# Mixer A of a two-layer trunk: left and right key tiles' blocks folded by a minimum before the exponential and put apart by GpSimd, and q and k split straight from PSUM

## The chip, the cores and the metric

The kernel is one program on one core of a Trainium2 chip. The metric is the time in device microseconds (us) of one execution. The core has five engines that run their own instruction lists and wait for each other by semaphores: PE (TensorE: matrix products, and transposes as a product with a unit matrix), DVE (VectorE), ACT (ScalarE), POOL (GpSimd) and SP (SyncE, which here only issues transfers). PE writes its results into PSUM, a small memory from which DVE and ACT read them; everything else lies in SBUF.

## The reference, cut to what matters

The trunk has two layers on 1024 tokens of width 1024 (a grid of 16 rows and 64 columns). The change touches only mixer A, the first layer's attention over a neighbourhood: each query sees a window of 8 rows and 16 columns around it.

```
def mixer_a(h, w_in, rpb, w_out):
    proj = h @ w_in
    q, k, v, gate = jnp.split(proj, 4, axis=-1)          # 16 heads of 64
    ...
    bias = rpb[:, dr[:, None, :, None], dc[None, :, None, :]]
    ...
        kg = jnp.take(k, flat, axis=2)...                 # the 8 x 16 window's keys
        sc = jnp.einsum('bhqd,bhqnd->bhqn', qb, kg).astype(jnp.float32) * scale
        sc = sc + bb.astype(jnp.float32)[None]
        pr = jax.nn.softmax(sc, axis=-1).astype(vg.dtype)
        return jnp.einsum('bhqn,bhqnd->bhqd', pr, vg)
    ...
    return (o * jax.nn.silu(gate)) @ w_out
```

## The kernel before, in words

The tokens are laid out as 8 tiles of 128: tile j holds 8 columns of the grid with their 16 rows. With a window of 16 columns, the queries of tile j find their keys in the tiles j-1, j and j+1 (the inner tiles j = 1 to 6) or in two tiles (j = 0 and 7). Within the left and the right tile, a query's window takes complementary columns: a key column that counts on the left does not count on the right.

Every matrix product of fp32 numbers is made as three products of high and low parts (`split3`, `mm` on line 317), so each operand is first split: ACT writes the rounded high part, DVE subtracts it from the original and writes the low part.

Mixer A is one long stretch of the span. It goes through 128 steps, 16 heads h by 8 query tiles j, and step n = (h, j) issues in this order: a head (a Y finish `fin` on POOL if one is due; at j = 1 the five POOL operations of `table(h+1)`, line 681; at other j one job, a DMA issued by POOL or SP), then

- `f_T(n)`: PE transposes the three 128 x 128 blocks of exponentials `sp` into PSUM tile `t` (line 723), ACT evacuates the high part into `PTh` (line 726), DVE the low part into `PTl` (line 727); both buffers have a slot for each pair of key and query tile;
- `f_E(n+1)`: ACT exponentials over 384 columns, in place in `sp` (line 715);
- `f_S(n+2)`: PE scores into `s`, 384 columns, and one DVE instruction that adds mask and bias and takes the row minimum (line 706);
- `f_AV(n-2)`: PE products of V with three slots of `PTh`, then of `PTl`, into `o`. In the heads 3, 7 and 11 each of them is followed by one tile of the v projection (`v_items`, 24 matmuls of 256 columns into a tile `d`, evacuated by ACT line 633 and DVE line 634).

`mix()` deals the dense work between these items by a cost table: in each head 8 items of the next head's q and k projection (two halves, each with a PSUM tile `d` of its own, 24 matmuls of 512 columns) and 4 items of the gate projection (one `d`). All of these share the two buffers of the PSUM pool `pd`. After every item `pulse()` runs: it pumps the weight queue (which loads `wstage` and has ACT line 226 and DVE line 231 split it into `wh` and `wl`) and counts down `post`, a list of things to issue so many pulses later. Each engine works through its list in the order in which the program issues it.

When a half of q and k stands in `d`, `qk_evac` copies it to SBUF (`th`, line 647) and splits it from there in three posted parts, after 2, 5 and 8 pulses (`QD = (2, 5, 8)`): ACT q high and k high (650, 651), then DVE q low and k low (654, 655) and a copy of k high to the other 64 partitions (656), then the copy of k low (659). For head 0 all of it is issued at once.

The Y path of a head pair is joined on ACT and DVE (lines 497 and 461), its reciprocals go through DRAM and come back as `rb` by two transfers of SP (line 470), and `fin` multiplies on POOL: by the gate (line 531), then by `rb` (line 532). Of the finishes, 14 lie on steps of mixer A, at j = 3 and j = 6 of the even heads.

Of the kernel before, what the change touches and what calls it, by code (L numbers as in the profile page):

```python
# [11 lines left out]
F32 = mybir.dt.float32  # L12
F32R = mybir.dt.float32r
# [74 lines left out]
def lay_out(inp):  # L88
# [46 lines left out]
    ok = np.stack([rowok, left, rowok, right, rowok], axis=1)  # L135
    mask = np.where(ok, 0.0, BIG).astype(np.float32)

    inv = np.power(np.float32(10000.0), -np.arange(16, dtype=np.float32) * np.float32(2.0) / np.float32(32.0)).astype(np.float32)
# [7 lines left out]
    def swap(v):  # L146
# [5 lines left out]
        "x": tokens(g["x"][0]), "wts": W, "rpb": rpb, "gains": gains, "hgains": hg,  # L152
        "mask": mask, "rope": np.stack([cosT, sinT], axis=1),
        "gain0": gains[0].reshape(8, 128).T,
# [3 lines left out]
@with_exitstack  # L158
def trunk(ctx, tc, x, wts, rpb, gains, hgains, mask, rope, gain0, out):
    nc = tc.nc  # L160
# [446 lines left out]
    def mixer_a():  # L607
        jobs = weight_sums()
        with ExitStack() as es:
# [27 lines left out]
            def qk_evac(h, hf):  # L637
                def evac(ps):
                    if hf == 0:
                        QS[h] = qkp.tile([128, 1024], F32R, name="QS")  # L640
                        KA[h] = qkp.tile([128, 1024], F32R, name="KA")
                        KB[h] = qkp.tile([128, 1024], F32R, name="KB")
                    s = slice(hf * 512, (hf + 1) * 512)
                    lo, hi = slice(0, 64), slice(64, 128)
                    qs, ka, kb = QS[h], KA[h], KB[h]
                    raw = sb.tile([128, 512], F32, name="th", bufs=2)
                    act.activation(raw, ps, AF.Copy)

                    def one():
                        act.activation(qs[lo, s], raw[lo], AF.Copy, scale=-0.125)  # L650
                        act.activation(ka[hi, s], raw[hi], AF.Copy)

                    def two():
                        dve.scalar_tensor_tensor(qs[hi, s], raw[lo], -0.125, qs[lo, s], op0=ALU.mult, op1=ALU.subtract)
                        dve.tensor_tensor(kb[hi, s], raw[hi], ka[hi, s], ALU.subtract)
                        dve.tensor_copy(ka[lo, s], ka[hi, s])
# [29 lines left out]
            def near(j):  # L686
                return max(j - 1, 0), min(j + 1, NT - 1)

            def f_S(h, j):
# [12 lines left out]
                else:  # L702
# [5 lines left out]
                                         scale=1.0, scalar=1e38, op0=ALU.add, op1=ALU.min, accum_out=mn)  # L708
                SP[h, j] = (sp, mn)

            def f_E(h, j):
                k0, k1 = near(j)
                n = (k1 - k0 + 1) * 128
                sp, mn = SP[h, j]
                act.activation(sp[:, :n], sp[:, :n], AF.Exp, bias=mn, scale=-1.0, accum_out=RS[h][:, j:j + 1])

            def f_T(h, j):
                k0, k1 = near(j)
                m = k1 - k0 + 1
                sp, _ = SP.pop((h, j))  # L720
                ps = psT.tile([128, 4, 128], F32, name="t")
                for i in range(m):
                    pe.transpose(ps[:, i], sp[:, i * 128:(i + 1) * 128], ident)
                f0 = k0 * 3 + (j - k0 + 1)
                sl = slice(f0, f0 + 2 * m - 1, 2)
                act.activation(PTh[:, sl], ps[:, :m], AF.Copy)  # L726
                dve.tensor_tensor(PTl[:, sl], ps[:, :m], PTh[:, sl], ALU.subtract)  # L727

# [125 lines left out]
            newton(4)  # L854
            sync.dma_start(MK, mask)
            for c in range(8):
                sync.dma_start(U[:, c], rpb[:, :, 7 - c:31 - c])
# [27 lines left out]
            ptp = es.enter_context(tc.tile_pool(name="ptp", bufs=1))  # L885
            PTh = ptp.tile([128, NT * 3, 128], F32R, name="PTh")
            PTl = ptp.tile([128, NT * 3, 128], F32R, name="PTl")
            for d in qk_items(0):
# [20 lines left out]
            for h in range(NH):  # L909
                att = []  # L910
                for j in range(NT):
# [783 lines left out]

NAMES = ["x", "wts", "rpb", "gains", "hgains", "mask", "rope", "gain0"]

# [14 lines left out]
```

## Time and profile before

| what | value |
|---|---|
| median of 3 runs | 1530.34 us (1529.68 to 1532.05) |
| profiled execution's own time | 1530.75 us |
| its span | 1529.0 us (1.75 us lie outside) |
| PE, DVE, ACT, POOL busy | 98%, 72%, 59%, 20% of the span |
| granted TensorE clock, mean | 0.999 |
| mixer A's steps | about 70 to 520 us of the span |

The profile is of one execution. Busy time counts an engine as busy while an instruction of it runs; a matmul's end is modelled, so PE's starts tell more than its durations: where matmuls start every 0.23 us without a gap, PE is full, though each is shown as lasting 0.39. "Idle before" and the waits name the instruction whose end let an engine go on. The dense phase, mixer B and the last dense phase follow mixer A; the change does not touch them.

### The profile page before, as it was taken

How to read it: one execution, taken by the hardware profiler on the slowest of the kernel's cores; microseconds unless marked ns; L12 is line 12 of the kernel's file. 1: busy time of each engine (PE TensorE's matmuls, PEld its weight loads, DVE VectorE, ACT ScalarE, POOL GpSimd, SP SyncE). 2: the span in 40 equal slices, each digit the busy share in tenths (PEclk: the TensorE clock that was granted, in tenths of full speed). 3: DMA queues.
4: the chain of work that ended last, by engine and by line, in shares of the span. 5: the costliest groups of instructions: out<-in, count | busy, mean ns of one | idle time of the engine just before them, and what ended most of it. 6: DMA issues, size and time to landing. Idle time of an engine off the chain costs nothing.

```text
span 1529.0 us, 24364 instructions
## 1 busy us (share of the span) xinstructions
PE 1499.0 (98%) x8976; PEld 1312.1 (86%) x8976; DVE 1099.1 (72%) x2091; ACT 899.6 (59%) x1801; POOL 305.0 (20%) x413
## 2 busy tenths in 40 slices
PE   9999999999999999999999999999999999999997
PEld 8888988988988887888988889989899888778786
DVE  7666576477477499767877786777877777689856
ACT  6565465466366635433567776666767777744432
POOL 1222232242112000010312132443131300000022
PEclk9999999999999999999999999999999999999999
DMA  8325355262122863262210111111111122663123
GB/s 261 129 85 135 83 142 162 63 169 80 36 87 73 327 247 97 90 203 79 75 49 22 32 40 49 46 32 51 49 32 43 45 69 81 226 224 114 67 88 134
DMA packets 91096, 157.22 MB, mean 103 GB/s; under 512 B 18144, under 2 KB 54112, under 8 KB 90464
## 3 DMA queue, kind: packets, MB, share of 16 engines
q1 hardware_dynamic: 85824, 139.66, 27.4%
q0 software_dynamic: 2560, 8.39, 3.1%
q10 hardware_dynamic: 2592, 7.61, 1.4%
q8 instruction: 71, 1.16, 0.3%
q14 instruction: 49, 0.40, 0.1%
HBM read 125.10 MB, written 50.83 MB: 115 GB/s over the span
## 4 chain that ended last, share of the span: by engine, by line
PE 36%; DVE 10%; ACT 4%; issue 3%; DMA 0%; SPq 0%; ACTq 0%; DVEq 0%
PE d L317 17%; PE o L317 7%; PE t L1178 5%; PE s L317 5%; DVE PTl L1181 2%; DVE mn L1162 1%; ACT P L1168 1%; ACT PTh L1180 1%; PE t L317 1%; DVE xn L1498 1%; DVE QS L1142 0%; DVE wl L231 0%; DVE X L1394 0%; PE t L1132 0%; ACT wh L226 0%
## 5 line engine op out<-in xcount | busy, mean ns | idle before, releaser
L317 PE MATMUL d<-wh,HTh 128*128 128x256 f32 (+1 forms) x1032 | 343.0, 334 | 3.6 <-ACT HTh L446 0.8
L317 PE MATMUL d<-wh,HTl 128*128 128x256 f32 (+1 forms) x1032 | 337.9, 329 | 0.3 <-DVE HTl L447 0.3
L317 PE MATMUL d<-wl,HTh 128*128 128x256 f32 (+1 forms) x1032 | 337.2, 329 | 0.0
L1181 DVE TENSOR_TENSOR PTl<-t,PTh 128x512 fp32r<-128x512 f32 x256 | 164.4, 684 | 111.6 <-ACT PTh L1180 111.2
L317 PEld LDWEIGHTS d<-wh,HTh 128*128 128x128 f32 x1032 | 194.6, 189 | 24.3 <-ACT HTh L446 1.2
L317 PEld LDWEIGHTS d<-wl,HTh 128*128 128x128 f32 x1032 | 194.8, 190 | 18.9
L317 PEld LDWEIGHTS d<-wh,HTl 128*128 128x128 f32 x1032 | 194.7, 190 | 18.7 <-DVE HTl L447 0.5
L317 PE MATMUL d<-HTh,wh 128*128 128x512 f32 x504 | 206.0, 409 | 0.0
L317 PE MATMUL d<-HTh,wl 128*128 128x512 f32 x504 | 198.4, 394 | 0.0
L317 PE MATMUL d<-HTl,wh 128*128 128x512 f32 x504 | 197.6, 392 | 0.0
L1168 ACT ACTIVATE P<-s,mn 128x1024 f32<-128x1024 f32 x128 | 142.7, 1115 | 59.7 <-DVE mn L1162 59.0
L1180 ACT ACTIVATE PTh<-t 128x512 fp32r<-128x512 f32 x256 | 140.0, 593 | 44.6 <-PE t L1178 44.3
L1162 DVE TENSOR_REDUCE mn<-s 128x1 f32<-128x1024 f32 x128 | 154.8, 1210 | 12.3 <-PE s L317 12.2
L1178 PE MATMUL t<-ident,P 128*128 128x128 f32 x1024 | 137.6, 275 | 6.1 <-DVE PTl L1181 4.0
L317 PE MATMUL s<-KA,QS 128*128 128x512 f32 (+2 forms) x384 | 133.8, 402 | 0.0
L1178 PEld LDWEIGHTS t<-ident,P 128*128 128x128 f32 x1024 | 114.6, 140 | 21.9 <-DVE PTl L1181 15.9
L231 DVE TENSOR_TENSOR wl<-wstage,wh 128x1024 fp32r<-128x1024 f32 x78 | 101.0, 1300 | 35.6 <-ACT wh L226 35.1
L317 PE MATMUL s<-KB,QS 128*128 128x512 f32 (+2 forms) x384 | 121.8, 371 | 0.0
L727 DVE TENSOR_TENSOR PTl<-t,PTh 128x384 fp32r<-128x384 f32 (+1 forms) x128 | 66.6, 521 | 74.5 <-ACT PTh L726 73.3
L317 PE MATMUL o<-PTh,V 128*128 128x256 f32 (+2 forms) x672 | 118.9, 288 | 1.2 <-DVE Y L461 0.9
L317 PE MATMUL o<-PTl,V 128*128 128x256 f32 (+2 forms) x672 | 119.1, 288 | 0.1
L317 PEld LDWEIGHTS d<-HTh,wl 128*128 128x128 f32 x504 | 94.7, 188 | 21.5
(237 smaller groups left out, 2698.5 us busy)
## 6 DMA issues: line engine op xcount, KB each, us to landing
wstage<-in_wts SPq DMA_DIRECT2D x88, 512.0 KB
pp<-ppD SPq DMA_DIRECT2D x32, 256.0 KB
X<-in_x SPq DMA_DIRECT2D x15, 512.0 KB
rb<-rD SPq DMA_DIRECT2D x56, 128.0 KB
ppD<-th SPq DMA_DIRECT2D x20, 256.0 KB
tD0t<-in_wts SPq DMA_DIRECT2D x16, 256.0 KB
tD1t<-in_wts SPq DMA_DIRECT2D x16, 256.0 KB
xD<-X SPq DMA_DIRECT2D x8, 512.0 KB
```

The costliest lines, as they stand in the source:

```text
L231: eng.tensor_tensor(lo[:, c:c + n], s[:, c:c + n], hi[:, c:c + n], ALU.subtract)
L317: pe.matmul(ps, a, b, start=first, stop=last, skip_group_check=True)
L727: dve.tensor_tensor(PTl[:, sl], ps[:, :m], PTh[:, sl], ALU.subtract)
L1162: dve.tensor_reduce(mn, ps, axis=AX.X, op=ALU.min)
L1168: act.activation(p, ps, AF.Exp, bias=mn, scale=-1.0, accum_out=RS[h, hf][:, t:t + 1])
L1178: pe.transpose(ps[:, i], p[:, k * 128:(k + 1) * 128], ident)
L1180: act.activation(PTh[:, ks, c], ps, AF.Copy)
L1181: dve.tensor_tensor(PTl[:, ks, c], ps, PTh[:, ks, c], ALU.subtract)
L1498: dve.scalar_tensor_tensor(xn, X[t], rn[m][:, i:i + 1], g1, op0=ALU.mult, op1=ALU.mult)
```

## The change

It has three parts, all in mixer A.

**Fold.** For the inner tiles, DVE takes after line 708 (706 before) the minimum of the left and the right 128 x 128 block, into the left one (line 713). A masked score is very large, so the minimum keeps the one of the two that counts. Exponentials run over 256 columns instead of 384, PE makes two transposes instead of three, and the evacuations (731, 732) take 256 columns. The folded block goes into a spare slot, and two POOL operations (line 736, `apart`, one for `PTh`, one for `PTl`) multiply it with the two halves of a 0/1 mask `SIDE` into its left and right slots. `f_AV` runs three steps behind instead of two, and reads what POOL wrote.

**q and k.** No copy `th`: ACT writes q high and k high straight from PSUM `d` (648, 649) when the half is complete. DVE's two subtractions (`lows`, 652 and 653), 2 pulses later, read `d` as well, so that `d` is held until they end. The two DVE copies become two transfers within SBUF issued by SP (660), 5 pulses later.

**Input.** `sides`, loaded once into `SIDE`.

```diff
+            SIDE = one.tile([128, 2, 128], F32, name="SIDE")
...
-                    raw = sb.tile([128, 512], F32, name="th", bufs=2)
-                    act.activation(raw, ps, AF.Copy)
-
-                    def one():
-                        act.activation(qs[lo, s], raw[lo], AF.Copy, scale=-0.125)
-                        act.activation(ka[hi, s], raw[hi], AF.Copy)
-
-                    def two():
-                        dve.scalar_tensor_tensor(qs[hi, s], raw[lo], -0.125, qs[lo, s], op0=ALU.mult, op1=ALU.subtract)
-                        dve.tensor_tensor(kb[hi, s], raw[hi], ka[hi, s], ALU.subtract)
-                        dve.tensor_copy(ka[lo, s], ka[hi, s])
-
-                    def three():
-                        dve.tensor_copy(kb[lo, s], kb[hi, s])
-                    for i, f in enumerate((one, two, three)):
-                        if h == 0:
-                            f()
-                        else:
-                            post.add(QD[i], f)
+                    act.activation(qs[lo, s], ps[lo], AF.Copy, scale=-0.125)
+                    act.activation(ka[hi, s], ps[hi], AF.Copy)
+
+                    def lows():
+                        dve.scalar_tensor_tensor(qs[hi, s], ps[lo], -0.125, qs[lo, s], op0=ALU.mult, op1=ALU.subtract)
+                        dve.tensor_tensor(kb[hi, s], ps[hi], ka[hi, s], ALU.subtract)
+
+                    def across():
+                        for k in (ka, kb):
+                            if h == 0:
+                                dve.tensor_copy(k[lo, s], k[hi, s])
+                            else:
+                                sync.dma_start(k[lo, s].bitcast(F32), k[hi, s].bitcast(F32))
+                    if h == 0:
+                        lows()
+                        across()
+                    else:
+                        post.add(QD[0], lows)
+                        post.add(QD[1], across)
...
+                if 0 < j < NT - 1:
+                    dve.tensor_tensor(sp[:, 0:128], sp[:, 0:128], sp[:, 256:384], ALU.min)
...
+                n = 256
                 act.activation(sp[:, :n], sp[:, :n], AF.Exp, bias=mn, scale=-1.0, accum_out=RS[h][:, j:j + 1])
...
-                for i in range(m):
-                    pe.transpose(ps[:, i], sp[:, i * 128:(i + 1) * 128], ident)
...
-                act.activation(PTh[:, sl], ps[:, :m], AF.Copy)
-                dve.tensor_tensor(PTl[:, sl], ps[:, :m], PTh[:, sl], ALU.subtract)
+                inner = 0 < j < NT - 1
+                for i in range(2):
+                    c = 1 - i if inner else i
+                    pe.transpose(ps[:, i], sp[:, c * 128:(c + 1) * 128], ident)
+                k0 = near(j)[0]
+                f0 = 3 * j + 1 if inner else k0 * 3 + (j - k0 + 1)
+                f1 = 3 * NT + j % 2 if inner else f0 + 2
+                sl = slice(f0, f1 + 1, f1 - f0)
+                act.activation(PTh[:, sl], ps[:, :2], AF.Copy)
+                dve.tensor_tensor(PTl[:, sl], ps[:, :2], PTh[:, sl], ALU.subtract)
+                if inner:
+                    def apart():
+                        for pt in (PTh, PTl):
+                            pool.tensor_tensor(pt[:, 3 * j - 1:3 * j + 4:4], pt[:, f1:f1 + 1].to_broadcast([128, 2, 128]), SIDE,
+                                               ALU.mult)
+                    apart()
...
-                    if n >= 2:
-                        att += av_and_v(*steps[n - 2])
+                    if n >= 3:
+                        att += av_and_v(*steps[n - 3])
...
-                    att += [(lambda: f_AV(NH - 1, NT - 2), CA[4]), (lambda: f_AV(NH - 1, NT - 1), CA[4])]
+                    att += [(lambda k=k: f_AV(NH - 1, k), CA[4]) for k in range(NT - 3, NT)]
```

The change moves instructions at three places that matter below. The first is DVE's list in head 3, at steps (3,4) to (3,6), where v tiles are projected. Before, the splits read the copy `th_1727`:

```order
L706 ISA mn_1719 128x1
L231 TENSOR_TENSOR wl1_1732<-wstage_1262,wh1_1731 128x1024
L634 TENSOR_TENSOR V_107<-d_1734,V_107 128x4x64
L727 TENSOR_TENSOR PTl_636<-t_1769,PTh_635 128x3x128
L654 TENSOR_SCALAR QS_1590<-th_1727,QS_1590 64x512
L655 TENSOR_TENSOR KB_1592<-th_1727,KA_1591 64x512
L656 COPY KA_1591<-KA_1591 64x512
```

Now, with the PSUM tile `d_1631` of q and k in the place of the copy:

```order
L708 ISA mn_1719 128x1
L713 TENSOR_TENSOR sp_1718<-sp_1718 128x128
L232 TENSOR_TENSOR wl1_1733<-wstage_1265,wh1_1732 128x1024
L652 TENSOR_SCALAR QS_1609<-d_1631,QS_1609 64x512
L653 TENSOR_TENSOR KB_1611<-d_1631,KA_1610 64x512
L636 TENSOR_TENSOR V_107<-d_1735,V_107 128x4x64
L732 TENSOR_TENSOR PTl_638<-t_1770,PTh_637 128x2x128
```

The subtractions moved ahead of the next V and PTl, still stand behind the weight split `wl`, and the buffer of `d_1631` comes free only behind them.

The second place is PE's list there, with the first matmul of the gate projection's tile, which takes that buffer. Before (`t_1769` are the transposes of step (3,6); x3 counts them):

```order
L317 MATMUL d_1734<-wh1_1417,HTh_73 128x256
L317 MATMUL d_1734<-wl1_1418,HTh_73 128x256
L317 MATMUL d_1734<-wh1_1417,HTl_74 128x256
L723 MATMUL t_1769<-ident_68,sp_1669 128x128 x3
L317 MATMUL d_1779<-HTh_73,wh1_858 128x512
L317 MATMUL d_1779<-HTl_74,wh1_858 128x512
```

Now:

```order
L318 MATMUL d_1735<-wh1_1433,HTh_73 128x256
L318 MATMUL d_1735<-wl1_1434,HTh_73 128x256
L318 MATMUL d_1735<-wh1_1433,HTl_74 128x256
L726 MATMUL t_1770<-ident_68,sp_1666 128x128 x2
L318 MATMUL d_1780<-HTh_73,wh1_859 128x512
L318 MATMUL d_1780<-HTl_74,wh1_859 128x512
```

The matmul on `d_1779` waited for ACT, which ends the copy `th`; that on `d_1780` waits for DVE, which ends the subtractions. In the same way the last v tile, `d_2106` at (4,3), waits for the subtractions on `d_1948`. Behind the last q and k matmul PE now has, up to it:

```order
L726 MATMUL t_2080<-ident_68,sp_1967 128x128 x2
L318 MATMUL s_2090<-KA_1610,QS_1609 128x384
L318 MATMUL s_2090<-KB_1611,QS_1609 128x384
L318 MATMUL d_2097<-HTh_73,wh1_1732 128x512
L318 MATMUL d_2097<-HTl_74,wh1_1732 128x512
L318 MATMUL d_2097<-HTh_73,wl1_1733 128x512
L318 MATMUL d_2097<-HTh_73,wh1_1732 128x512
L318 MATMUL d_2097<-HTl_74,wh1_1732 128x512
L318 MATMUL d_2097<-HTh_73,wl1_1733 128x512
L318 MATMUL o_1852<-PTh_637,V_107 128x256
L318 MATMUL o_1852<-PTl_638,V_107 128x256
L318 MATMUL d_2106<-wh1_1241,HTh_73 128x256
```

This work is all that PE has between the end of the one tile and the wait; ACT has in that time the two high parts from `d_1948` and then `PTh` from `t_2080`, and DVE has `PTl` from `t_2080` ahead of the two subtractions. Both places come again in the heads 7/8 and 11/12.

The third place is POOL's list around the two finishes of head 4. Before, tables and finishes stand in a row:

```order
L681 TENSOR_TENSOR tb_2009<-MK_108,u_1765 128x128 x5
L531 TENSOR_TENSOR Y_1488<-Y_1488,G_1511 128x512
L532 TENSOR_TENSOR Y_1488<-Y_1488,rb_1489 128x512
L597 DMA tD0t3_82<-in_wts 64x1024 x2
L597 DMA tD0t2_81<-tD0t1_80 64x1024
L531 TENSOR_TENSOR Y_1578<-Y_1578,G_1903 128x512
```

Now the `apart` pairs of the steps stand between them:

```order
L736 TENSOR_TENSOR PTh_637<-PTh_637,SIDE_109 128x2x128
L736 TENSOR_TENSOR PTl_638<-PTl_638,SIDE_109 128x2x128
L532 TENSOR_TENSOR Y_1535<-Y_1535,G_1522 128x512
L533 TENSOR_TENSOR Y_1535<-Y_1535,rb_1536 128x512
L598 DMA tD0t3_82<-in_wts 64x1024
L736 TENSOR_TENSOR PTh_637<-PTh_637,SIDE_109 128x2x128
L736 TENSOR_TENSOR PTl_638<-PTl_638,SIDE_109 128x2x128
L598 DMA tD0t2_81<-tD0t1_80 64x1024
```

A finish and a job stand between the pair of step (4,2) and that of step (4,3), and PE's products of step (4,5) need the latter.

More of the change, by code (lines that the diff above doesn't have):

```diff
@@ L152, in lay_out @@
         "x": tokens(g["x"][0]), "wts": W, "rpb": rpb, "gains": gains, "hgains": hg,
-        "mask": mask, "rope": np.stack([cosT, sinT], axis=1),
+        "mask": mask, "sides": sides, "rope": np.stack([cosT, sinT], axis=1),
         "gain0": gains[0].reshape(8, 128).T,
@@ L158, in trunk @@
 @with_exitstack
-def trunk(ctx, tc, x, wts, rpb, gains, hgains, mask, rope, gain0, out):
+def trunk(ctx, tc, x, wts, rpb, gains, hgains, mask, sides, rope, gain0, out):
     nc = tc.nc
@@ L855, in mixer_a @@
             sync.dma_start(MK, mask)
+            sync.dma_start(SIDE, sides)
             for c in range(8):
@@ L885, in mixer_a @@
             ptp = es.enter_context(tc.tile_pool(name="ptp", bufs=1))
-            PTh = ptp.tile([128, NT * 3, 128], F32R, name="PTh")
-            PTl = ptp.tile([128, NT * 3, 128], F32R, name="PTl")
+            PTh = ptp.tile([128, NT * 3 + 2, 128], F32R, name="PTh")
+            PTl = ptp.tile([128, NT * 3 + 2, 128], F32R, name="PTl")
             for d in qk_items(0):
@@ L1693, in trunk @@
     dense_phase(1)
-NAMES = ["x", "wts", "rpb", "gains", "hgains", "mask", "rope", "gain0"]
+NAMES = ["x", "wts", "rpb", "gains", "hgains", "mask", "sides", "rope", "gain0"]
 def kernel(**inputs):
```

7 lines of the change are left out of this document (1 added, 6 removed).

## The prediction

> **What bounds the kernel now.** I read the page first, then the stretch of mixer A by windows, then the waits there, and last the timeline of single steps. The page says that PE is nearly full over the whole span:
>
> ```profile
> PE 1499.0 (98%) x8976; PEld 1312.1 (86%) x8976; DVE 1099.1 (72%) x2091; ACT 899.6 (59%) x1801; POOL 305.0 (20%) x413
> ```
>
> That is an average, so the stage decides. The window from 85 to 480 us lies within mixer A; its columns are the length and the busy times of PE, weight loads, DVE, ACT and POOL, then the granted clock and the DMA share:
>
> ```profile
> 85.00:480.00 395.00, 394.58 (x2301) 347.55 (x2300) 249.22 (x559) 226.47 (x507) 101.98 (x124) 1.00 0.37 103
> ```
>
> PE is idle for 0.42 of 395 us, at the full clock, while DVE works 63% and ACT 57% of the time. The waits from 50 to 527 us (total, times, longest) show who waits:
>
> ```profile
> POOL tb L681 <- DVE mn L706: 168.6, 9, 29.6
> PEld t L723 <- ACT sp L715: 6.7, 19, 1.1
> PE t L723 <- ACT sp L715: 1.0, 2, 0.8
> ```
>
> PE's own longest row is 1.0 us, and no row has PE waiting for a buffer `d`. POOL waits much, but for leave to run ahead. So in this stage each us of PE work that goes is a us gained, each us for which PE stands is a us lost, and what ACT, DVE or POOL save is worth nothing by itself.
>
> **The fold: PE's saving.** One step's PE instructions show what they cost, by the distance of their starts:
>
> ```profile
> 210.00 0.49 PE L723 MATMUL t<-ident,sp 128*128 128x128 f32 x3
> 210.24 0.48 PE L317 MATMUL d<-HTh,wh 128*128 128x512 f32 x1
> 210.56 0.40 PE L317 MATMUL d<-HTl,wh 128*128 128x512 f32 x1
> 210.79 0.39 PE L317 MATMUL d<-HTh,wl 128*128 128x512 f32 x1
> ...
> 211.71 0.34 PE L317 MATMUL s<-KA,QS 128*128 128x384 f32 x1
> 211.88 0.34 PE L317 MATMUL s<-KB,QS 128*128 128x384 f32 x1
> 212.06 0.34 PE L317 MATMUL o<-PTh,V 128*128 128x384 f32 x1
> ```
>
> A matmul of 512 columns takes 0.23 (210.56 to 210.79), one of 384 columns 0.175. From 210.00 to 210.56 there are three transposes and one matmul `d`: 0.56 - 0.23 = 0.33, so 0.11 for a transpose. The change drops one in 16 heads x 6 inner tiles = 96 steps: 96 x 0.11 = **10.6 us of PE**. Nothing else of PE's work changes.
>
> **The fold: what else gets shorter or longer.** The groups by form show the other engines' rows (busy, mean ns):
>
> ```profile
> L715 ACT ACTIVATE sp<-sp,mn 128x384 f32<-128x384 f32 x96 | 58.9, 614 | 8.1 <-DVE mn L706 7.5
> L715 ACT ACTIVATE sp<-sp,mn 128x256 f32<-128x256 f32 x32 | 16.2, 505 | 6.4 <-DVE mn L706 6.4
> L726 ACT ACTIVATE PTh<-t 128x384 fp32r<-128x384 f32 x96 | 47.1, 490 | 56.3 <-PE t L723 55.5 <-PE d L317 0.3
> L726 ACT ACTIVATE PTh<-t 128x256 fp32r<-128x256 f32 x32 | 12.2, 383 | 10.6 <-PE t L723 10.3
> L727 DVE TENSOR_TENSOR PTl<-t,PTh 128x256 fp32r<-128x256 f32 x32 | 13.2, 413 | 10.3 <-ACT PTh L726 10.0
> L997 DVE TENSOR_TENSOR qt<-th,tab x8: 283/284/500, 718.3 to 739.0; 128x128 f32<-128x128 f32 x8
> L997 POOL TENSOR_TENSOR qt<-qt,tab x24: 725/739/1219, 782.0 to 1200.0; 128x256 f32<-128x256 f32 x24
> L997 POOL TENSOR_TENSOR qt<-th,tab x8: 449/463/466, 935.7 to 981.7; 128x128 f32<-128x128 f32 x8
> ```
>
> ACT saves 0.109 on an exponential and 0.107 on `PTh`: 96 x 0.216 = 20.7 us, none of it on the path. The minimum is new on DVE; the nearest row is mixer B's 128x128 operation of two SBUF inputs, 0.284 (0.5 at most). It lengthens the way from scores to exponentials, which has a whole step to run in: by the waits above transposes come late by 7.7 us in all today, and 0.11 of the 0.284 comes back in the exponential. I put it at nothing; if that cover were gone it would cost 96 x 0.17 = 16 us.
>
> An `apart` operation moves 256 columns on POOL; the nearest row is mixer B's of that width, 0.739, up to 1.219. A pair takes 1.48, 96 pairs 142 us beside the 102 that POOL has in the window. That fits, but PE now waits for it. The products trail by three steps instead of two for that, and a step is two to four us long, as the first ACT instruction of steps (2,2), (2,3) and (2,4) shows, with POOL's finish beside them:
>
> ```profile
> 111.60 0.49 ACT L726 ACTIVATE PTh<-t 128x384 fp32r<-128x384 f32 x1
> 113.87 0.49 ACT L726 ACTIVATE PTh<-t 128x384 fp32r<-128x384 f32 x1
> 117.52 0.49 ACT L726 ACTIVATE PTh<-t 128x384 fp32r<-128x384 f32 x1 [1.90 <-PE t L723]
> 111.57 1.30 POOL L532 TENSOR_TENSOR Y<-Y,rb 128x512 f32<-128x512 f32 x1 [6.49 <-DMA rb<-rD]
> 113.47 1.30 POOL L531 TENSOR_TENSOR Y<-Y,G 128x512 f32<-128x512 f32 x1 [0.60 <-DVE Y L461]
> L597 POOL DMA_DIRECT2D tD0t<-tD0t x8 | 7.1, 1100 | 3.2 <-DMA tD0t<-tD0t 3.2
> ```
>
> In a plain step the pair is done 0.4 + 1.48 after that ACT start, two steps ahead of its use. In the 14 steps with a finish the list is: pair of (2,2) until 111.60 + 1.9 = 113.5, two multiplies of 1.30 until 116.1, a job of 1.1 until 117.2, pair of (2,3) until 118.7. Its use is in step (2,5), which by the steps' distances (2.3, 3.65, then again about 2.3) starts at about 119.4. That is 0.7 spare, and another us or so until the products' turn within the step. But `rb` itself, landed at 111.57 here, comes one step later too (the products that end the head trail more): 2.3 to 3.7, which brings the second multiply to 114 to 115.4, so no or half a us of delay. I take **1 us** for all 14, between 0 and 6.
>
> By the Trainium skill's page "GPSIMD Engine Reference", section 4.1 Engine selection, an elementwise operation of two inputs belongs on VectorE, with GpSimd about twice as slow. It speaks against `apart`; the 128x128 rows of line 997 bear it out (0.283 on DVE, 0.463 on POOL, 1.6 times). By the page alone, with twice DVE's 0.283 for 128 columns, a pair of 256 columns would be 2.3 and the list at a finish 1.6 longer, 0.9 past its spare: an estimate of 12 us more.
>
> **q and k: the held buffer.** The copies go, off the path, but `d` now comes free behind the second subtraction instead of behind the copy. Where PE has much to do before it takes the buffer again, this hides; in plain heads it has the next half's or the gate's 24 matmuls and several steps' work. In heads 3/4, 7/8 and 11/12 the v tiles take the same two buffers, and two places come out short in each. The rows for it:
>
> ```profile
> 207.46 0.40 PE L317 MATMUL d<-HTh,wl 128*128 128x512 f32 x1
> 207.90 0.60 ACT L647 ACTIVATE th<-d 128x512 f32<-128x512 f32 x1 [0.74 <-PE d L317]
> 157.58 0.28 PE L317 MATMUL d<-wl,HTh 128*128 128x256 f32 x1
> 157.70 0.28 PE L317 MATMUL d<-wh,HTl 128*128 128x256 f32 x1
> L497 ACT ACTIVATE Y<-o 64x512 f32<-64x512 f32 x64 | 38.0, 594 | 24.8 <-PE o L317 19.4 <-issue 4.5
> L461 DVE SCALAR_TENSOR_TENSOR Y<-o,Y 64x512 f32<-64x512 f32 x64 | 43.5, 680 | 6.9 <-ACT Y L497 5.5
> L656 DVE CAST KA<-KA 64x512 fp32r<-64x512 f32 x32 | 15.2, 476 | 1.0
> L226 ACT ACTIVATE wh<-wstage 128x1024 fp32r<-128x1024 f32 x81 | 84.6, 1051 | 3.1 <-DMA wstage<-in_wts 3.1
> L231 DVE TENSOR_TENSOR wl<-wstage,wh 128x1024 fp32r<-128x1024 f32 x78 | 101.0, 1300 | 35.6 <-ACT wh L226 35.1
> ```
>
> What goes is ACT's 0.60 and DVE's 0.476, and as much again for k low, per half. What stays: the last matmul's start to ACT's start is 0.44; 64x512 from PSUM costs ACT 0.594 and DVE 0.680; a matmul of 256 columns starts every 0.12.
>
> - The gate's tile at (3,6): DVE has the weight split ahead of the subtractions. 0.44 + 2 x 0.594 + 1.05 (`wh`) + 1.30 (`wl`) + 2 x 0.68 + about 0.1 between engines = 5.44. PE has the last matmul 0.23, two products 0.35, 24 v matmuls 2.88, two transposes 0.22: 3.68. PE stands 1.76.
> - The last v tile at (4,3): 0.44 + 2 x 0.594 + `PTh` 0.383 + `PTl` 0.413 + 2 x 0.68 + 0.1 = 3.88. PE has one matmul and six more of 512 columns 1.61, two transposes 0.22, two scores 0.35, two products 0.24: 2.42. PE stands 1.46.
>
> Three times 3.22 is 9.7; since neighbouring instructions overlap by up to 0.1 of what is shown, I take **9.4 us**. The bounds are 0 (the same buffer is taken without a wait today) and 3 x 2 x 2.7 = 16, with `wl` doubled at one place and the subtractions stretched.
>
> By the Trainium skill's page "Perfetto Trace Analysis", section Matmuls, independent groups should rotate through PSUM banks so that the evacuation of one overlaps the next group's matmuls. Today's trace agrees (no wait on `d`); with two buffers and a later release, that rule speaks against this part, and it would have the change without it at 10.6 less 1, 9.6 us faster.
>
> K's repeat is hidden: after the subtractions PE has over 9 us of work in the order before the next head's scores, and a 128 KB transfer of SP's today is issued in 1.13 and has landed within 3.8 (107.80 to 111.57):
>
> ```profile
> 107.80 1.13 SPq L470 DMA_DIRECT2D rb<-rD  x2
> ```
>
> The `rb` transfers and the weight loads queue behind it on SP; 60 more issues, each half of 1.13, are 34 us of SP's time in mixer A's 450. If that cover is gone, each us costs 15.
>
> **Sum.** Against the profiled run's 1530.75 us (span 1529.0 and 1.75 around it; 0.4 over the median of 1530.34, so they are taken as one): -10.6 + 9.4 + 1.0 = -0.2, so 1530.5, which I give as **1531**. A measurement of this kernel can tell about 0.2%, 3 us, from no change.
>
> **The rivals.**
>
> A, the saving stands. The waits for `d` come out at a third, because DVE is ahead of its list (37% idle) and issues the split `wl` before the subtractions are due; POOL hides. For it: no engine but PE is near full. Against it: both chains start at PE's last matmul, so idle time ahead of them does not help. -10.6 + 3.1 gives 1523.3.
>
> B, slower: POOL comes late at the finishes. If `apart` takes 1.219, the highest of its row, the list of the two pairs at a finish is 4 x 0.48 = 1.9 longer; less the spare of 0.7, each of 14 finishes costs 1.2 of PE: 16 to 17 us more, 1547. It decides as soon as an operation takes over 0.739 + 0.7/4 = 0.91. For it, POOL's rows in mixer A range widely:
>
> ```profile
> L681 POOL TENSOR_TENSOR tb<-MK,u x80: 451/640/1992, 42.4 to 465.7; 128x128 f32<-128x128 f32 x80
> ```
>
> Against it, DVE's instructions here mostly read PSUM, and the products stand late in their step. By the Trainium skill's page "SBUF — State Buffer", section Who interferes with whom, a DVE instruction with two SBUF inputs and a GpSimd one that reads SBUF exclude each other for a whole instruction; that would be this rival's cause, with the minimum and `wl` as the neighbours, and the row's 451 to 1992 agrees.
>
> C, slower: the K transfers land one us after their use in each of 15 heads, because SP's queue holds them behind a load that waits: 1546. For it, the DMA share of 0.37; against it, twice the time they need.
>
> **How the numbers follow.** The main case has 0.47, its own range 1527 to 1536 (waits of 6 to 13 us, POOL 0 to 2): of it 0.04 is faster, 0.31 within 0.2%, 0.12 slower. A has 0.26 (0.25 faster, 0.01 same), B 0.20 (0.18 slower, 0.02 same), C 0.07 (slower). Together: faster 0.29, same 0.34, slower 0.37. The range leaves out the better third of A and what lies beyond three quarters of B and C: 1523 to 1543.
>
> **What would show it.** Right: 96 transposes fewer; PE rows waiting for DVE's line 653 on `d` of about 9 us, at six places; POOL busy by some 140 us more; `th` and the copies gone at no gain. Wrong: those waits under 3 us (A); PE's products `o` waiting for POOL's line 736 by over 5 us (B), or its scores for a DMA on `KA` or `KB` (C); or a time beyond the range with PE work that is not 10.6 us less.

## The result, and the profile after

The changed kernel takes 1549.83 us (median of 4, 1549.25 to 1550.95) against 1530.34 before: ratio 1.0123, 95% interval 1.0111 to 1.0136, so 19.5 us slower. 1531 was forecast, with a range up to 1543. The profiled execution's span is 1547.5 us, 18.5 more than before.

The page's first part, the window from 85 to 480 us (length, PE, weight loads, DVE, ACT, POOL, clock, DMA share), and PE's waits between 50 and 550 us (total, times, longest):

The page:

```profile
PE 1495.0 (97%) x8880; PEld 1303.7 (84%) x8880; DVE 1100.9 (71%) x2127; ACT 863.6 (56%) x1769; POOL 438.7 (28%) x605
```

The window:

```profile
85.00:480.00 395.00, 374.74 (x2137) 325.51 (x2136) 238.58 (x557) 188.69 (x461) 200.24 (x269) 1.00 0.46 118
```

The waits:

```profile
PE t L726 <- ACT sp L718: 13.0, 17, 1.4
PE d L318 <- DVE KB L653: 9.8, 6, 1.7
```

The 96 transposes are gone (8976 to 8880 matmuls), ACT has 36 us less to do over the span and DVE as much as before (1100.9 against 1099.1), and yet PE stands for 20.3 us in a window in which it stood for 0.4. Two waits show: the six for the PSUM buffer `d`, as forecast, and transposes that wait for exponentials, a row of 1.0 us before. No row has PE waiting for POOL.

Where in the span the time went is seen from the first and the last weight load of a transpose, before and after (durations, then first and last start). Before:

```profile
L723 PEld LDWEIGHTS t<-ident,sp x352: 137/139/144, 59.9 to 522.0; 128*128 128x128 f32 x176
```

After:

```profile
L726 PEld LDWEIGHTS t<-ident,sp x256: 137/139/145, 62.1 to 540.6; 128*128 128x128 f32 x128
```

From the first of these starts to the last, mixer A took 462.1 us and takes 478.5, 16.4 more (its steps begin at 59.9 us before, earlier than the "about 70" of the table further up). Behind it nothing changed (1529.0 - 522.0 = 1007.0, 1547.5 - 540.6 = 1006.9). Ahead of it are 2.2 us more; the first start lay between 59.9 and 61.9 in the runs below, with the old and the new q and k alike (67.0 and 67.7 in the two with scores three steps ahead), so I don't put it down to the change.

The waits of the view leave out part of what PE loses, since a matmul's shown end runs over the next one's start. So I added up, over the starts of PE's matmuls in mixer A, by how much each distance exceeds the pitch of its form, where that is over 0.1 us: ahead of transposes 17.9 us (30 places) against 2.2 (5), ahead of matmuls on `d` 11.6 (mainly the six places) against 0. So -10.6 + 15.7 + 11.6 = 16.7, beside 16.4 seen.

The largest of the late transposes come at the end of a head. DVE, ACT and PE there, in the timeline (start, duration):

```profile
123.98 1.22 DVE L530 TENSOR_TENSOR Y<-Y,rb 128x512 fp32r<-128x512 f32 x1
125.24 0.68 DVE L652 SCALAR_TENSOR_TENSOR QS<-d,QS 64x512 fp32r<-64x512 f32 x1
125.94 0.69 DVE L653 TENSOR_TENSOR KB<-d,KA 64x512 fp32r<-64x512 f32 x1
126.66 0.42 DVE L732 TENSOR_TENSOR PTl<-t,PTh 128x256 fp32r<-128x256 f32 x1
127.00 0.41 DVE L708 CUSTOM_DVE_ANT_1 sp<-s,tb 128x256 f32<-128x256 f32 x1
...
127.46 0.51 ACT L718 ACTIVATE sp<-sp,mn 128x256 f32<-128x256 f32 x1 [2.26 <-DVE mn L708]
...
126.48 0.28 PE L318 MATMUL o<-PTl,V 128*128 128x128 f32 x1
128.11 0.44 PE L726 MATMUL t<-ident,sp 128*128 128x128 f32 x2 [1.36 <-ACT sp L718]
```

ACT is idle for 2.26 us, waiting for a row minimum (line 708); DVE comes to it only behind the subtraction for Y's low part (line 530, DVE's half of the split of Y), the two subtractions of q and k and the `PTl` behind them. PE has nothing else and stands. Before, at the same pieces, the subtraction of Y stood a step earlier and those of q and k behind the row minimum:

```profile
118.04 0.69 DVE L529 TENSOR_TENSOR Y<-Y,rb 128x512 fp32r<-128x512 f32 x1
122.97 0.41 DVE L706 CUSTOM_DVE_ANT_1 sp<-s,tb 128x256 f32<-128x256 f32 x1
123.43 0.68 DVE L654 SCALAR_TENSOR_TENSOR QS<-th,QS 64x512 fp32r<-64x512 f32 x1
```

Ten such places make 11 of the 17.9 us: 1.5 us at the six where the subtraction of Y stands ahead of those of q and k, 0.45 at the four where it doesn't. What was off the path by its own length was on it by its place in an in-order list.

### The profile page after: what moved, and what is told of

It is laid out like the page before. It is cut to its first block, busy times and chain, and to the rows that moved or that the text cites. A ratio compares the mean times of both kernels' runs of the same rounds, so it can differ in the third digit from the quotient of the medians.

```text
span 1547.5 us, 24656 instructions
## 1 busy us (share of the span) xinstructions
PE 1495.0 (97%) x8880; PEld 1303.7 (84%) x8880; DVE 1100.9 (71%) x2127; ACT 863.6 (56%) x1769; POOL 438.7 (28%) x605
## 4 chain that ended last, share of the span: by engine, by line
PE 38%; DVE 9%; ACT 3%; issue 2%; ACTq 0%; DVEq 0%
PE d L318 18%; PE o L318 7%; PE t L1190 6%; PE s L318 6%; DVE PTl L1193 1%; DVE mn L1174 1%; ACT PTh L1192 1%; ACT P L1180 1%; PE t L318 1%; DVE xn L1510 1%; DVE X L1406 0%; PE t L1144 0%; DVE QS L1154 0%; DVE wl L232 0%; ACT wh L227 0%
## 5 line engine op out<-in xcount | busy, mean ns | idle before, releaser
L318 PEld LDWEIGHTS d<-wl,HTh 128*128 128x128 f32 x1032 | 195.0, 190 | 20.3 <-DVE wl L1304 1.4
L736 POOL TENSOR_TENSOR PTh<-PTh,SIDE 128x256 fp32r<-128x256 f32 x96 | 79.7, 830 | 205.3 <-ACT PTh L731 205.2
```

The source lines that it names most:

```text
L318: pe.matmul(ps, a, b, start=first, stop=last, skip_group_check=True)
L736: pool.tensor_tensor(pt[:, 3 * j - 1:3 * j + 4:4], pt[:, f1:f1 + 1].to_broadcast([128, 2, 128]), SIDE, ALU.mult)
```

## The experiments

All times are medians with the ratio to the kernel before, run on the same chip, and its 95% interval.

| kernel | us | ratio, interval |
|---|---|---|
| the fold alone (old q and k) | 1553.0 | 1.0139, 1.0124 to 1.0154 |
| q and k alone (no fold, lag 2) | 1559.7 | 1.0187, 1.0172 to 1.0202 |
| changed, copy put back | 1563.1 | 1.0207, 1.0190 to 1.0224 |
| the same, subtractions at 5 pulses | 1559.6 | 1.0182, 1.0167 to 1.0197 |
| changed, no apart | 1547.2 | 1.0109, 1.0092 to 1.0125 |
| fold alone, no apart | 1537.6 | 1.0042, 1.0027 to 1.0057 |
| fold alone, no apart, lag 2 | 1525.5 | 0.9962, 0.9949 to 0.9974 |
| changed, no apart, lag 2 | 1549.4 | 1.0124, 1.0108 to 1.0140 |
| before, lag 3 alone | 1544.2 | 1.0087, 1.0072 to 1.0102 |
| changed, subtractions at 4 pulses | 1557.6 | 1.0171, 1.0156 to 1.0186 |
| changed, scores 3 steps ahead | 1562.3 | 1.0204, 1.0174 to 1.0235 |
| fold alone, scores 3 steps ahead | 1547.2 | 1.0106, 1.0091 to 1.0121 |
| before, transfers of k alone | 1537.8 | 1.0039, 1.0025 to 1.0054 |
| before, high parts at once | 1550.3 | 1.0124, 1.0099 to 1.0150 |
| the same, subtractions at 2 pulses | 1573.0 | 1.0267, 1.0252 to 1.0282 |
| fold alone with apart, lag 2 | 1547.8 | 1.0107, 1.0092 to 1.0122 |

### Each half alone

The fold alone: `qk_evac` as before the change.

> The changed kernel with the q and k part undone: copy th, splits from it after 2, 5 and 8 pulses, DVE copies; the fold, POOL's apart and the third step of lag stay. Theory 1 (the q and k part does the harm: the buffer d held by DVE, 9.8 us, and the subtractions now 2 pulses behind the half, in DVE's list ahead of the next minimum, so that transposes come late, 11 us): 1549.8 - 9.8 - 11 = about 1529, or less if the other late transposes go too, at best 1530.3 - 10.6 = 1520. Theory 2 (the fold does the harm: the minimum on DVE, shown as 0.50 us beside POOL's work, makes exponentials and transposes late; only the 9.8 us of buffer waits belong to q and k): 1549.8 - 9.8 = 1540.

q and k alone: the kernel before with the new `qk_evac`.

> The kernel before with the q and k part alone (high parts and subtractions straight from PSUM, k repeated by transfers); three transposes, no POOL work on PTh and PTl, lag of two steps. Theory 1: both costs appear without the fold, 9.8 of buffer waits and about 11 of late transposes: 1530.3 + 21 = 1551, a few less where the third transpose gives DVE a little more time. Theory 2: only the buffer waits, 1540, and PE's waits for exponentials stay near the 1 us of before.

Both came out slower than the whole change, 1553.0 and 1559.7, and neither theory had that: each half costs over 20 us by itself, and together they cost 19.5. q and k alone has the buffer waits of the forecast (11.4 us at six places) and late transposes besides, without fold, lag or `apart`; so part of theory 1 stands. The fold alone has no buffer wait, and the most late transposes so far, 22 us of waits:

```profile
PE t L726 <- ACT sp L718: 22.0, 22, 3.1
```

Two runs between, with the copy put back into the changed kernel:

```diff
+                    raw = sb.tile([128, 512], F32, name="th", bufs=2)
+                    act.activation(raw, ps, AF.Copy)
-                    act.activation(qs[lo, s], ps[lo], AF.Copy, scale=-0.125)
+                    act.activation(qs[lo, s], raw[lo], AF.Copy, scale=-0.125)
... (and raw for ps in the other three)
-                        post.add(QD[0], lows)        # second run: QD[1], and across QD[2]
```

> The changed kernel with ACT's copy of the half to SBUF put back ahead of the splits, which read the copy; the subtractions stay 2 pulses behind, k goes by transfers. The buffer comes free behind the copy again. Both theories: the six waits for the buffer (9.8 us) go and the late transposes stay, 1540. If it stays near 1550, the buffer waits only hid other waits; if it comes near 1530, the late transposes came from the buffer.

> As the run with the copy put back, but the two subtractions 5 pulses behind the half (as before the change) and the transfers of k 8. It tells the place in DVE's list apart from the fold. Theory 1: buffer waits and the ten late transposes at the heads' ends both go, 1529 or less, near the run with the fold alone. Theory 2: as the run with the copy put back, 1540. If the transfers of k land too late, PE's scores wait for a DMA on KA or KB.

1563.1 and 1559.6, against 1529 to 1540 expected: the waits for the subtractions on `d` are gone, but the late transposes doubled (37 and 34 us by the starts). The subtractions, which now read SBUF, had become long: k low took 0.87 and 1.30 us, against 0.69 from PSUM in the changed kernel. That pointed to POOL. (ACT's copy, 0.60 us a half ahead of its other work, came back as well; these two runs don't tell the two apart.)

### POOL beside DVE

```diff
-                if inner:
+                if inner and h == 0:
                     def apart():
```

From the second head on, the folded block isn't put apart; PE reads the first head's blocks.

> The changed kernel with POOL's apart left out from the second head on (192 operations less 12; the products read what the first head left in those slots). DVE's list, PE's list and the lag stay. Theory 3 (POOL beside DVE: the 192 operations stretch DVE's instructions with two SBUF inputs, the minimum to 0.50 from 0.28, and so make exponentials and transposes late): the minimum falls to 0.28, the late transposes (18 us) mostly go, 1549.8 - 12 to 16 = 1534 to 1538, with the buffer waits of 9.8 left. Theory 4 (place in the lists: the subtractions ahead of the next minimum on DVE, the high parts ahead of the next exponential on ACT): the ten stalls at the heads' ends, 11 us, stand before minima of 256 columns without a fold and stay: 1545 to 1548.

> The run with the fold alone (q and k as before the change), with POOL's apart left out from the second head on in the same way. In the run with the fold alone DVE's splits of the copy th took 1.06 and 1.20 us instead of 0.73 and 0.78, the two copies 0.79 and 0.63 instead of 0.47 and 0.44. Theory 3: these rows fall back, the late transposes (27 us) go, and the saving of 10.6 us shows: 1520 to 1524. Theory 4 or the lag of three steps as the cause: well over 1530.

In the changed kernel the 180 POOL operations are worth 2.6 us at most; the intervals of the two ratios overlap. With the old q and k they are worth 15.4 (1553.0 to 1537.6). The groups of the fold alone with apart:

```profile
L713 DVE TENSOR_TENSOR sp<-sp 128x128 f32<-128x128 f32 x96 | 44.4, 463 | 3.3
L657 DVE TENSOR_TENSOR KB<-th,KA 64x512 fp32r<-64x512 f32 x32 | 37.4, 1169 | 0.5
L656 DVE SCALAR_TENSOR_TENSOR QS<-th,QS 64x512 fp32r<-64x512 f32 x32 | 33.2, 1036 | 5.2 <-ACT QS L652 4.2
L658 DVE CAST KA<-KA 64x512 fp32r<-64x512 f32 x32 | 24.5, 764 | 0.8
```

and without:

```profile
L713 DVE TENSOR_TENSOR sp<-sp 128x128 f32<-128x128 f32 x96 | 35.8, 372 | 3.3
L657 DVE TENSOR_TENSOR KB<-th,KA 64x512 fp32r<-64x512 f32 x32 | 23.8, 743 | 0.5
L656 DVE SCALAR_TENSOR_TENSOR QS<-th,QS 64x512 fp32r<-64x512 f32 x32 | 22.1, 689 | 4.4 <-ACT QS L652 3.6
L658 DVE CAST KA<-KA 64x512 fp32r<-64x512 f32 x32 | 14.3, 447 | 0.8
```

The splits and the copy of k high fall by a third or more, the fold's minimum (line 713) by a fifth. The copy of k low (line 661) does not: 0.619 us with `apart`, 0.634 without. In the changed kernel the subtractions read PSUM and are not stretched:

```profile
L652 DVE SCALAR_TENSOR_TENSOR QS<-d,QS 64x512 fp32r<-64x512 f32 x32 | 21.9, 684 | 5.5 <-ACT KA L649 4.6
L653 DVE TENSOR_TENSOR KB<-d,KA 64x512 fp32r<-64x512 f32 x32 | 22.2, 694 | 0.7
```

So the two halves of the change belong together: with POOL at work, q and k straight from PSUM by transfers avoid most of what the fold alone pays for `apart`. By the Trainium skill's page "SBUF — State Buffer", section Who interferes with whom, a DVE instruction with two SBUF inputs contends with a GpSimd instruction that reads SBUF, and one with at most one such input, outside the two-port modes, does not; the rows of the splits agree on both sides. Theory 3 explains 15.4 us of the fold alone and not the rest: its run came out at 1537.6 and not at 1520 to 1524. For the change itself theory 4 held, its 1545 to 1548 around 1547.2: the ten stalls at the heads' ends stayed, at 7.8 us instead of 11. What they lost lies at the six with the subtraction of Y, 1.0 us each instead of 1.5: it has two SBUF inputs and takes 0.68 or 0.69 there instead of 1.22.

Yet the fold alone without apart is still over the 1520 that its saving gives, by 17 us.

### The lag of three steps

```diff
-                    if n >= 3:
-                        att += av_and_v(*steps[n - 3])
+                    if n >= 2:
+                        att += av_and_v(*steps[n - 2])
```

> The run with the fold alone and without apart (1537.6), with the products two steps behind again instead of three. What is left of the change is the saving, 10.6 us of PE, and the minimum on DVE. If the lag of three steps costs time by itself (it moves the Y joins, which wait for the products, to other places in ACT's and DVE's lists): 1520 to 1524. If the lag costs nothing: 1537, and the fold's own shorter steps or the minimum make the transposes late.

> The kernel before with nothing changed but the products three steps behind instead of two. If the lag costs time by itself: 1540 or more, with transposes that wait for exponentials behind the Y joins. If not: 1531.

> The changed kernel without apart from the second head on (1547.2), with the products two steps behind. If the lag costs time by itself: 5 to 15 us less, 1532 to 1542, with the six buffer waits (about 10 us) left. If the place of the subtractions on DVE is what counts: 1545 to 1549, the stalls at the heads' ends stay.

The lag costs 12.1 us in the fold (1537.6 to 1525.5), and by itself, on the kernel before, 12.9 (1531.35, the median of before on that chip, to 1544.24). With lag 2 and without apart the fold brings 5.8 us, and PE is full again:

```profile
85.00:480.00 395.00, 394.02 (x2261) 345.18 (x2260) 270.39 (x656) 212.79 (x518) 101.70 (x124) 1.00 0.38 103
```

What the lag does is seen on ACT in head 2. Before (the same pieces at the same step):

```profile
119.75 1.05 ACT L226 ACTIVATE wh<-wstage 128x1024 fp32r<-128x1024 f32 x1
120.70 0.61 ACT L650 ACTIVATE QS<-th 64x512 fp32r<-64x512 f32 x1
121.32 0.63 ACT L651 ACTIVATE KA<-th 64x512 fp32r<-64x512 f32 x1
121.98 0.49 ACT L726 ACTIVATE PTh<-t 128x384 fp32r<-128x384 f32 x1
122.49 0.61 ACT L715 ACTIVATE sp<-sp,mn 128x384 f32<-128x384 f32 x1
```

With the lag alone:

```profile
121.74 1.05 ACT L226 ACTIVATE wh<-wstage 128x1024 fp32r<-128x1024 f32 x1
122.69 0.62 ACT L528 ACTIVATE rb<-Y 128x512 fp32r<-128x512 f32 x1
123.21 0.62 ACT L650 ACTIVATE QS<-th 64x512 fp32r<-64x512 f32 x1
123.84 0.63 ACT L651 ACTIVATE KA<-th 64x512 fp32r<-64x512 f32 x1
124.49 0.49 ACT L726 ACTIVATE PTh<-t 128x384 fp32r<-128x384 f32 x1
125.01 0.61 ACT L715 ACTIVATE sp<-sp,mn 128x384 f32<-128x384 f32 x1
...
125.77 0.33 PE L723 MATMUL t<-ident,sp 128*128 128x128 f32 x1 [0.52 <-ACT sp L715]
```

A head ends one step later, so the split of Y (line 528), posted so many pulses behind it, now falls between the weight split and q and k's high parts, and the evacuation and the exponential behind them come late. In the changed kernel without apart the lag made no difference in time (1547.2 and 1549.4), but not because the stalls at the heads' ends stayed, as the second case of the expectation had it. With the subtraction of Y a step earlier they fell from 7.8 us to 3.7 (0.3 or less at nine places, 1.2 at one behind a `wl` of 2.16), so of the 1.5 us about 0.3 belong to the subtractions of q and k, 0.7 to that of Y, which the lag put ahead of them, and 0.5 to its stretching beside POOL. Late transposes elsewhere made up for it (13.9 us in all against 15.4), and in that profile the granted clock was 0.50 for 3.4 us from 143.0 and from 269.3. What stays with either lag is the new q and k: against the fold with the old q and k (1525.5) they cost 24 us, by the starts 12.4 at `d` and 9.9 as late transposes.

### The place of q and k in the lists

High parts at once, and then also the subtractions and the two copies earlier, both from the copy and on the kernel before:

```diff
                     for i, f in enumerate((one, two, three)):
-                        if h == 0:
+                        if h == 0 or i == 0:
                             f()
                         else:
-                            post.add(QD[i], f)
+                            post.add(QD[i - 1], f)        # second run alone
```

> The kernel before with only the two high parts on ACT issued at once behind the copy, instead of 2 pulses later. If ACT's list, where they then stand ahead of an evacuation and an exponential that were due earlier, makes transposes late: 1534 to 1540, with PE waiting for exponentials. If ACT's 40% of idle time takes them: 1531.

> As the run with the high parts at once, and the two subtractions with the copy of k high 2 pulses behind the half, the other copy 5 (all from the copy th, so that the buffer d comes free as before). By the place in DVE's list: about 10 us over the run with the high parts at once, 1541 to 1550, with stalls of transposes at the heads' ends and none for the buffer. If only the held buffer counts: as that run.

1550.3 and 1573.0: the high parts two pulses sooner on ACT cost 18 us, about 4 of them in one stall behind a late store (see the transfers below), and the subtractions and copies three pulses sooner on DVE 23 more, with not one operation added. With the high parts at once, ACT and PE at the end of a half:

```profile
115.15 0.60 ACT L647 ACTIVATE th<-d 128x512 f32<-128x512 f32 x1 [0.79 <-PE d L317]
115.78 0.63 ACT L650 ACTIVATE QS<-th 64x512 fp32r<-64x512 f32 x1
116.42 0.63 ACT L651 ACTIVATE KA<-th 64x512 fp32r<-64x512 f32 x1
117.08 0.49 ACT L726 ACTIVATE PTh<-t 128x384 fp32r<-128x384 f32 x1
117.59 0.61 ACT L715 ACTIVATE sp<-sp,mn 128x384 f32<-128x384 f32 x1
...
118.35 0.44 PE L723 MATMUL t<-ident,sp 128*128 128x128 f32 x2 [0.94 <-ACT sp L715]
```

ACT stands 0.79 us waiting for the half's end, then works 1.9 us on it, and only then comes to what the next transpose needs. My bound for the high parts (nothing, or 1531) fell, and so did its upper end, 1540. For the second run 1541 to 1550 was expected, with stalls of transposes alone; PE also waited for `PTl` (5.4 us) and for the low parts of v tiles (3.3). In the changed kernel ACT has only the two high parts at this place, without the copy, so there the price can be lower.

In the changed kernel itself I moved the subtractions to 4 pulses (`QD = (4, 7, 8)`):

> The changed kernel with the subtractions 4 pulses behind the half instead of 2, and the transfers of k 7 instead of 5. Theory 4: the ten stalls of transposes at the heads' ends go or shrink (11 us), the six buffer waits grow by the PE work of two pulses each, 1 to 2 us: 1545 to 1551. Theory 3: the transposes' stalls stay as they are and the buffer waits grow: 1556 to 1562.

1557.6, theory 3's number, but not its reason: the stalls at the heads' ends stayed at 1.5 us because two pulses moved the subtractions only behind `PTl`, still ahead of the same minimum, while the waits on `d` grew (the longest from 1.7 to 2.9). By the starts the stalls grew by 3.7 us in all; as much again lies in two stretches, 187.5 to 194.3 and 447.0 to 450.4 us, in which the granted clock was 0.50 in this profile, and 1.00 in that of the changed kernel. The transfers of k, alone on the kernel before:

```diff
-                        dve.tensor_copy(ka[lo, s], ka[hi, s])
                     def three():
-                        dve.tensor_copy(kb[lo, s], kb[hi, s])
+                        for k in (ka, kb):
+                            ... sync.dma_start(k[lo, s].bitcast(F32), k[hi, s].bitcast(F32))
```

> The kernel before with only the two DVE copies of k replaced by SP's transfers within SBUF, 8 pulses behind the half. If the transfers do harm (SP's queue, or k late for the next head's scores): PE waits for a DMA on KA or KB, over 1535. If not, DVE has 27 us less to do off the path: 1530, or a little under 1531 where a minimum came late behind a copy.

1537.8, 6 us slower, though no score waits for k. Most of it is one stall of 4.0 us: ACT's join of Y waited for an earlier store of Y (`yD0h`) by SP.

```profile
ACT Y L497 <- DMA yD0h<-Y: 6.3, 1, 6.3
```

The kernel before has no such wait. It came in the run with the high parts at once too, 4.7 us, of which PE stood 4.1, and with q and k alone (6.9 us in two waits), so the transfers are not its only cause; what makes that store late stays open.

### Two ways out that weren't

Scores three steps ahead of the transposes (`f_S(n + 3)`, four buffers of `sp`), in the changed kernel and in the fold alone:

> The changed kernel with scores issued three steps ahead of the transposes instead of two (four buffers of sp instead of three); exponentials stay one step ahead. Every theory by which exponentials come late because DVE reaches the minimum late (3 and 4): the stalls of transposes (18 us) go, the buffer waits of 9.8 stay, 1534. If scores then wait for q and k of the next head (DVE's subtractions or the transfers), PE waits for s instead and the time stays.

> The run with the fold alone, with scores issued three steps ahead of the transposes (four buffers of sp). If late minima on DVE are what makes transposes late (27 us in the run with the fold alone), they go, and with k copied by DVE and not sent by transfers the next head's scores may find it in time: 1553 - 27 = 1526, under the kernel before. If scores then wait for q and k, as 9 us did in the changed kernel with this lead: 1535 to 1545.

1562.3 and 1547.2. In the changed kernel the stalls of transposes fell from 17.9 to 8.0 us by the starts, as every theory wanted, but PE's scores then wait for the next head's k (6.2 us for `KA`'s transfer), and mixer A's first transpose comes 5 us later. The fold alone won 6 us. And the fold with apart, lag of two:

> The fold with POOL's apart, q and k as before the change, and the products two steps behind: 1525.5 without apart. POOL's stretching of DVE's splits of the copy cost 15.4 with the lag of three: 1541, and PE's products wait for POOL at the 14 finishes, 1 to 3 us each, 14 to 40 more: 1555 to 1580. If PE doesn't wait for POOL, 1541 or less, and the third step of lag was not needed.

1547.8, better than with the lag of three (1553.0) and than the 1555 to 1580 expected:

```profile
PE o L318 <- POOL PTl L736: 9.6, 15, 1.5
PE o L318 <- POOL PTh L736: 5.8, 7, 1.3
```

PE does wait for POOL here, 15.4 us, which the lag of three steps avoids, and the lag costs about as much. No kernel that computes the whole reference came out under the kernel before; the only one below it leaves apart out.

## Why the prediction was wrong, point by point

**The saving: right.** 96 transposes went. In the one run that leaves PE full (fold, no apart, lag 2) mixer A's window has 1.0 us of idle PE in 395, and the kernel is 5.8 us under before; of the 4.8 that lack to 10.6, 2.2 are PE's waits for the `apart` left in the first head.

**The held buffer: right in place and size.** Six places, 9.8 us by the waits and 11.6 by the starts, against 9.4 forecast. 1.7 us for the gate's tile and 1.6 for the last v tile by the waits, 1.76 and 1.46 forecast.

**apart: right that it hides, wrong that it costs nothing beside.** PE never waits for POOL in the changed kernel, where an `apart` operation takes 0.81 us on average, under rival B's 0.91; B's time of 1547 was near the result by luck, for a cause that did not happen. But POOL's work stretches DVE's instructions on SBUF, 15.4 us with the old q and k, up to 2.6 with the new. Of the terms, the fold's minimum was taken at 0.284 and measured 0.497 in the changed kernel, 0.384 without apart.

**The step that failed** is the one that put the way from scores through exponentials to transposes at nothing: "It lengthens the way from scores to exponentials, which has a whole step to run in. [...] I put it at nothing". It asked only what the fold's minimum adds to that way, and about the minimum it was right: with minimum and old lists (fold, no apart, lag 2) transposes come late by 4.0 us by the starts, against 2.2 before. It did not ask what the rest of the change puts ahead of the row minima and exponentials. The third step of lag stands in the prediction only as cover for `apart`, and of q and k only the held buffer has a term, the rest is "off the path". The slack was taken from lengths of chains and busy shares (DVE 63%, ACT 57%) and not from the lists: which instruction stands ahead of each row minimum and each exponential.

The change moved the high parts 2 pulses and the subtractions 3 pulses forward and the Y path one step back. On the kernel before, the runs show a cost for each: 18 us for the high parts (4 of them the late store), 23 more for the subtractions with the copies, 12.9 for the lag. In the changed kernel they overlap and come to 15.7 us of late transposes; how these divide between high parts, subtractions and lag is shown at the heads' ends alone. The bound written for a lost cover, 16 us, has that size by chance: it was the minimum's, and it was not put in the range.

K's repeat was hidden from the scores, as forecast. Rival A fell: DVE's idle time did not help, as was said against it.

## What to carry to other kernels

Where one engine is full and the others feed it in order, an off-path instruction costs by its place: write down, for each thing that the full engine waits for, what stands ahead of it in the feeding engine's list before and after the change, with what each of those waits for. A lag or an earlier issue is an edit to every list it passes, and is priced last, by a run of it alone. Work given to GpSimd beside a busy VectorE is best judged together with where VectorE's operands lie: from PSUM they kept their time.

## What the runs showed of the hardware that was not expected

A DVE copy with one SBUF input (line 658) was stretched beside POOL like the splits with two, 0.764 against 0.447 us, though the like copy of line 661 was not longer with `apart` than without (0.619 and 0.634), and from PSUM 0.684 and 0.694 held. The granted clock in the window from 50 to 85 us, where PE stands for some us at the start of mixer A, was 0.95 in the fold alone (first row) and 1.00 without apart and with the lag of two (second row; the clock is the third number from the end):

```profile
50.00:85.00 35.00, 29.97 (x144) 24.66 (x143) 23.53 (x52) 18.99 (x43) 14.62 (x22) 0.95 0.32 116
```

and

```profile
50.00:85.00 35.00, 31.50 (x157) 25.58 (x156) 25.80 (x55) 20.59 (x45) 14.17 (x22) 1.00 0.35 123
```

PE is idle for 5.0 and 3.5 us there; it was 0.90 with 3.5 in the fold without apart, so idle time alone doesn't tell. In finer windows the clock is 0.50 from 68.1 to 71.5 us in the fold alone and from 66.8 to 73.6 without apart, and by the starts each of the two has a single stall of 3.2 us there (ending at 68.6 and 67.8), while the run with the lag of two has none over 1.7. The fold alone has three more such stretches of 3.4 us, from 201.2, 327.5 and 453.8, each at the end of a stall of 2.3 to 2.8. The changed kernel, whose longest stall is 1.9, has none between 50 and 540 us. But a stall of 2.8 in the run with subtractions at 4 pulses had none behind it, so what decides stays open.
